# Residual rows of x put straight into the four result tiles of the output stage

## The chip, the cores and the metric

The kernel runs on one core of one Trainium2 chip. The metric is the device time of one execution in microseconds (us). Times inside a profile are counted from the start of its span, which is the time from the first to the last recorded instruction; the execution's own time is a little longer than its span.

## What is computed

One inference step of a one-layer decoder for a prompt of 512 rows and 32 sample rows (8 sequences of 4), each row 1024 wide. Two branches (windowed attention, gated delta rule) are projected, gated and merged; the change lies behind all of that, in the last two lines of the layer:

```python
merged = sigmoid(ga) * (ya @ w_branch_a) + sigmoid(gb) * (yb @ w_branch_b)
r  = ALPHA * x + gate * (merged @ w_out)          # merged: 544 x 1024, w_out: 1024 x 1024
mu = mean(r); var = mean((r - mu)**2)             # over the 1024 columns of a row
y  = (r - mu) * rsqrt(var + LN_EPS) * ln_g + ln_b
```

All values are fp32. Products are made of three passes over high and low parts (high by high, high by low, low by high).

## The kernel before

**How the order comes about.** The kernel first records every operation with the tiles that it reads and writes, and then sets the order of each of five queues with a planner. The queues are TensorE (PE), VectorE (DVE), ScalarE (ACT), GpSimd (POOL) and SyncE (SP), which issues the DMAs. The planner walks through time by its own cost table. On each queue it takes, among the operations whose inputs it reckons ready, the one with the lowest (rank, place in the program). On the chip each queue then runs in that fixed order: an instruction that waits holds back everything behind it on its engine. All recorded operations carry the line L728 in the profile, so they are told apart by their tiles.

**The output stage.** The merged rows stand as `mhi[k]` and `mlo[k]` (eight blocks of 128 columns, high and low part), the weights as `wo0h`, `wo0l` (columns 0 to 511, called half 0 here) and `wo1h`, `wo1l` (half 1). `product_out` makes one product of a block of 128 rows (tt = 0 to 3) and a half n: 24 matmuls of 512 columns into one tile `pp`. There are two `pp` buffers, so PE can begin a product only when the product two before it has been read out of its buffer by DVE. The loop at the end of `body` goes through the products in the order (0,0), (1,0), (2,0), the sample rows, (0,1), (1,1), (2,1), (3,0) and (3,1); the last one is split in two products of 256 columns, called (3,1a) and (3,1b) here.

For each product, `load_x` has SP load 128 x 512 values of x into a tile `xr` and ACT scale them by ALPHA. DVE then writes half the gated product into the result tile `r[tt]` (a `SCALAR_TENSOR_TENSOR r<-pp,gp`) and adds `xr` to it (a `TENSOR_TENSOR r<-r,xr`). `xr` comes from the pool `o2` with two buffers, so a load can begin only when the add two loads before it is done.

When both halves of a block are there, `norm_out` normalises the row. For blocks 0 to 2 ACT makes the mean and the variance (`sq,mv<-r` twice, with small steps between); for block 3 DVE does so (`BN_STATS`, `BN_AGGR`). DVE then subtracts the mean and multiplies by `lng` (1024 columns, `r<-r,mv,lng`), takes a reciprocal, and multiplies and adds `lnb` in two halves (`r<-r,mv,lnb`), each followed by its store to `y_p`. Block 3 has a lower rank number, so it goes ahead of other work that is ready.

`samples_out` handles the 32 sample rows, spread over 128 partitions with 256 columns each. Its loads are `xs`, `lns` and `quarter`; two tiny matmuls with `quarter` (tile `pd`) sum up means and variances and stand in PE's queue between the matmuls of other products.

Of the kernel before, what the change touches and what calls it, by code (L numbers as in the profile page):

```python
# [11 lines left out]
F32 = mybir.dt.float32  # L12
F32R = mybir.dt.float32r
AF = mybir.ActivationFunctionType
OP = mybir.AluOpType
# [4 lines left out]
D = 1024  # L20
# [14 lines left out]
ALPHA = 2.0 ** 0.25  # L35
# [215 lines left out]
class Recorder:  # L251
# [21 lines left out]
    def pool(self, make, name, bufs, side):  # L273
        return Pool(self, make, name, bufs, side)
# [506 lines left out]
def body(ctx, tc, io):  # L781
    rec = Recorder()
    pe, ve, se, ge, sp = rec.engines()
# [104 lines left out]
    n = CONST[2].shape[1]  # L888
# [8 lines left out]
    with ExitStack() as fctx:  # L897
# [65 lines left out]
        for b, (c, m) in enumerate(CHUNKS):  # L963
# [3 lines left out]
            for k in range(c, c + m):  # L967
                se.activation(x1[0][:, k, :SEQ], xT[:, k, :SEQ], AF.Copy, scale=sc[:, k, 0:1])
                if k == c:
# [4 lines left out]
                                        op0=OP.mult, op1=OP.subtract)  # L974
# [3 lines left out]
            for k in range(c, c + m):  # L978
                for t in range(3):
                    w, w_ = (x[:, k - c, 128 * t:128 * t + 128] for x in (hi, lo))  # L980
# [24 lines left out]
        with rec.together():  # L1005
            for k in range(KT):
                q = k % 4
# [1244 lines left out]
    gp = al.tile([128, D], F32, name="gp")  # L2252
# [5 lines left out]
    def out_rows(n, k):  # L2258
        return io["w_out"][k * 128:k * 128 + 256, 512 * n:512 * n + 512].rearrange("(a p) c -> p a c", a=2)

    def load_out(n):

        for k in range(0, KT, 2):
            raw = (wraw if n == 0 or k < 6 else o1).tile([128, 2, 512], F32, name="wo", **({"tag": "wraw"} if n == 0 or k < 6 else {}))
            sp.dma_start(raw, out_rows(n, k))
            plain[n, k] = raw
            se.activation(wo[n][0][:, k:k + 2], raw, AF.Copy)
            ve.tensor_sub(wo[n][1][:, k:k + 2], raw, wo[n][0][:, k:k + 2].bitcast(F32))
# [28 lines left out]
    o1 = pool(ox, "o1", 1, "right")  # L2297
    o2 = pool(ox, "o2", 2, "right")
    wo.append([o1.tile([128, KT, 512], F32R, name=f"wo1{u}") for u in "hl"])
    load_out(1)  # L2300
    lng = o1.tile([128, D], F32, name="lng")
    sp.dma_start(lng, io["ln_g"].to_broadcast([128, D]))
    lnb = o1.tile([128, D], F32, name="lnb")
    sp.dma_start(lnb, io["ln_b"].to_broadcast([128, D]))
    for k in range(0, KT, 2):
        name = ("hi", "lo")[k // 4]
# [7 lines left out]
            sp.dma_start(lns[32 * q:32 * q + 32, i], io[n][:, 256 * q:256 * q + 256].to_broadcast([32, 256]))  # L2314
    quarter = o1.tile([128, 128], F32, name="quarter")
    sp.dma_start(quarter, io["const_q"])
    r = [o1.tile([128, D if tt < 4 else 256], F32, name=f"r{tt}") for tt in range(5)]
    bn, bns = o1.tile([128, 4, 6], F32, name="bn"), o1.tile([128, 6], F32, name="bns")
    parts = lambda k: ((mhi[k], 0), (mhi[k], 1), (mlo[k], 0))

    def product_out(tt, c0, c1):
        n, w = c0 // 512, slice(c0 % 512, c0 % 512 + c1 - c0)
        po = pp()[:, 0:c1 - c0]
        for k in range(KT):
            for i, (a, b) in enumerate(parts(k)):
                pe.matmul(po, a[:, 128 * tt:128 * tt + 128], wo[n][b][:, k, w],
                          start=(k == 0 and i == 0), stop=(k == 7 and i == 2))
        return po

    def load_x(tt, n):  # L2330
        xr = o2.tile([128, 512], F32, name="xr")
        sp.dma_start(xr, io["x"][128 * tt:128 * tt + 128, 512 * n:512 * n + 512])
        se.activation(xr, xr, AF.Copy, scale=ALPHA)
        return xr

    def norm_out(tt, mv=None):
        q = r[tt]
        if mv is None:
            mv, sq = o2.tile([128, 4], F32, name="mv"), o1.tile([128, D], F32, name="sq")
            se.activation(sq, q, AF.Copy, scale=1.0 / D, accum_out=mv[:, 0:1])  # L2340
            se.activation(mv[:, 3:4], mv[:, 0:1], AF.Copy, scale=-1.0)
            se.activation(sq, q, AF.Square, bias=mv[:, 3:4], accum_out=mv[:, 1:2])
            se.activation(mv[:, 2:3], mv[:, 1:2], AF.Sqrt, bias=eps5, scale=1.0 / D)
        else:
            se.activation(mv[:, 2:3], mv[:, 1:2], AF.Sqrt, bias=eps5)
        ve.scalar_tensor_tensor(q, q, mv[:, 0:1], lng, op0=OP.subtract, op1=OP.mult)
        ve.reciprocal(mv[:, 2:3], mv[:, 2:3])
        for w in (slice(0, 512), slice(512, 1024)):
            ve.scalar_tensor_tensor(q[:, w], q[:, w], mv[:, 2:3], lnb[:, w], op0=OP.mult, op1=OP.add)
            sp.dma_start(io["y_p"][128 * tt:128 * tt + 128, w], q[:, w])  # L2350

    def samples_out():
        xr = o1.tile([128, 256], F32, name="xs")
        for b in range(4):
            sp.dma_start(xr[32 * b:32 * b + 32], io["x"][SEQ:NT, 256 * b:256 * b + 256])
        se.activation(xr, xr, AF.Copy, scale=ALPHA)
        po = pp()
        with rec.together():
            for k in range(KT):
                for q in range(4):  # L2360
                    n, c = divmod(256 * q, 512)
                    pe.matmul(po[32 * q:32 * q + 32, 0:256], ms[:, k], plain[n, k // 2 * 2][:, k % 2, c:c + 256],
                              start=(k == 0), stop=(k == 7), tile_position=(0, 32 * q))
        q = r[4]
        ve.scalar_tensor_tensor(q, po[:, 0:256], 0.5, gs, op0=OP.mult, op1=OP.mult)
        ve.tensor_add(q, q, xr)
        ve.bn_stats(bns, q)
        mv = o2.tile([128, 4], F32, name="mv")
        ve.bn_aggr(mv[:, 0:2], bns)
        pm = pd()  # L2370
        pe.matmul(pm[:, 0:1], quarter, mv[:, 0:1], start=True, stop=True)
        se.activation(mv[:, 2:3], pm[:, 0:1], AF.Square, bias=mv[:, 0:1], scale=-1.0)
        ve.tensor_add(mv[:, 1:2], mv[:, 1:2], mv[:, 2:3])
        pe.matmul(pm[:, 1:2], quarter, mv[:, 1:2], start=True, stop=True)
        se.activation(mv[:, 3:4], pm[:, 1:2], AF.Sqrt, bias=eps5)
        ve.tensor_copy(mv[:, 2:3], pm[:, 0:1])
        ve.scalar_tensor_tensor(q, q, mv[:, 2:3], lns[:, 0], op0=OP.subtract, op1=OP.mult)
        ve.reciprocal(mv[:, 3:4], mv[:, 3:4])
        ve.scalar_tensor_tensor(q, q, mv[:, 3:4], lns[:, 1], op0=OP.mult, op1=OP.add)
        for b in range(4):  # L2380
            sp.dma_start(io["y_s"][:, 256 * b:256 * b + 256], q[32 * b:32 * b + 32])

    for tt, n in ((0, 0), (1, 0), (2, 0), (None, 0), (0, 1), (1, 1), (2, 1), (3, 0), (3, 1)):
        if tt is None:
            samples_out()
            continue
        xr, q = load_x(tt, n), r[tt]
        step = 256 if n and tt == 3 else 512
        for c in range(512 * n, 512 * n + 512, step):
            po = product_out(tt, c, c + step)  # L2390
            w = slice(c, c + step)
            at_end = tt == 3 and c == 768
            rec.rank = -2 * (n and tt == 3)
            with rec.together() if at_end else nullcontext():
                ve.scalar_tensor_tensor(q[:, w], po, 0.5, gp[:, w], op0=OP.mult, op1=OP.mult)
                ve.tensor_add(q[:, w], q[:, w], xr[:, c - 512 * n:c - 512 * n + step])
                if tt == 3:
                    for i in range(c // 256, (c + step) // 256):
                        ve.bn_stats(bn[:, i, :], q[:, 256 * i:256 * i + 256])
                if at_end:  # L2400
                    mv = o2.tile([128, 4], F32, name="mv")
                    ve.bn_aggr(mv[:, 0:2], bn.rearrange("p a b -> p (a b)"))
            rec.rank = 0
        if n:
            rec.rank = -2 * (tt == 3)
            norm_out(tt, mv if tt == 3 else None)
            rec.rank = 0
# [112 lines left out]
```

## Time and profile before

| what | value |
|---|---|
| median of 3 runs (lowest to highest) | 882.32 us (881.55 to 884.74) |
| time of the profiled execution | 881.68 us |
| its span | 879.9 us |
| instructions in the span | 20682 |
| busy: PE, PE weight loads, DVE, ACT, POOL | 98%, 92%, 73%, 51%, 8% |
| mean granted TensorE clock | 0.995 |
| output stage, first product read out to the end of the span | 828.54 to 879.9 us |

Rows of the timeline give start, duration, engine, line, operation, output<-inputs, shapes and count; a bracket at the end tells how long the engine had been idle before, and what ended that. Rows with xN merge N neighbours. SPq rows are DMA issues: their duration is the issue, not the transfer. In a row of the windows, each engine has its busy time and its instructions, then come the granted clock, the share of time that the 16 DMA engines were busy, and GB/s.

### The profile page before, as it was taken

To read this page: it belongs to the slowest core of one execution; us is meant where nothing else is said; L and a number is where in the kernel's file an instruction comes from. 1 tells how busy PE (TensorE), PEld (TensorE's weight loads), DVE (VectorE), ACT (ScalarE), POOL (GpSimd) and SP (SyncE) were. 2 spreads that over 40 slices of the span, in tenths; PEclk is the share of its full clock that TensorE was granted. 3 is DMA by queue.
4 is the path that set the end of the run, shared out by engine and by line. 5 is a ranking of instruction groups with operands and counts; after the bars stand their busy time and mean duration, and the time that the engine had idled before them with its cause. 6 is when DMAs were issued, how large, how long until landed. Compare 5 with 4: busy or idle time off the path is not lost.

```text
span 879.9 us, 20682 instructions
## 1 busy us (share of the span) xinstructions
PE 859.4 (98%) x8152; PEld 811.3 (92%) x8152; DVE 643.4 (73%) x1328; ACT 452.0 (51%) x1073; POOL 70.2 (8%) x167
## 2 busy tenths in 40 slices
PE   8999999999999999999999999999999999999995
PEld 7889999898999899999999998999999999999874
DVE  4776557565448999867999853556999699998547
ACT  3556656765546796347785446732442222334333
POOL 0120110110001110001020000021010000001000
PEclk9999999999999999999999999999999999999998
DMA  9976769656687887899878796479969799987974
GB/s 331 348 218 205 232 205 285 227 194 224 191 262 253 276 275 205 269 288 305 303 227 283 238 303 216 171 214 300 345 213 381 271 412 417 372 293 238 342 250 153
DMA packets 121069, 236.18 MB, mean 268 GB/s; under 512 B 49174, under 2 KB 76640, under 8 KB 118284
## 3 DMA queue, kind: packets, MB, share of 16 engines
q1 hardware_dynamic: 120972, 234.86, 79.6%
q8 instruction: 64, 1.05, 0.5%
q14 instruction: 33, 0.27, 0.1%
HBM read 218.53 MB, written 103.97 MB: 367 GB/s over the span
## 4 chain that ended last, share of the span: by engine, by line
PE 79%; DVE 7%; DMA 6%; ACT 5%; issue 1%; SPq 1%; POOL 0%; DVEq 0%; ACTq 0%
PE pp L728 60%; PE pg L728 8%; PE pd L728 7%; PE pb L728 4%; ACT L728 1%; DMA wv<-dw 1%; DMA slab<-in_ks 1%; DMA dO<-orow 1%; ACT hi L728 1%; DMA bias<-in_bias_p 1%; DVE r L728 1%; ACT sq L728 1%; DVE acc L728 1%; DMA wc<-in_w_cb 1%; DMA S<-in_state_delta 1%
## 5 line engine op out<-in xcount | busy, mean ns | idle before, releaser
L728 PE MATMUL pp<-hhi,hi 128*128 128x272 f32 x1360 | 397.6, 292 | 2.0 <-DVE zt L728 1.3
L728 PE MATMUL pp<-hhi,lo 128*128 128x272 f32 x1360 | 397.3, 292 | 0.0
L728 PE MATMUL pp<-hlo,hi 128*128 128x272 f32 x1360 | 395.7, 291 | 0.0
L728 PEld LDWEIGHTS pp<-hhi,hi 128*128 128x128 f32 x1360 | 256.4, 189 | 4.9 <-issue 1.8
L728 PEld LDWEIGHTS pp<-hhi,lo 128*128 128x128 f32 x1360 | 256.4, 189 | 2.1 <-issue 1.4
L728 PEld LDWEIGHTS pp<-hlo,hi 128*128 128x128 f32 x1360 | 256.3, 188 | 1.4 <-issue 0.4
L728 ACT ACTIVATE hi<-wt 128x1024 fp32r<-128x1024 f32 (+1 forms) x101 | 103.5, 1025 | 169.4 <-PE pp L728 138.3
L728 DVE TENSOR_TENSOR lo<-wt,hi 128x1024 fp32r<-128x1024 f32 (+1 forms) x101 | 118.9, 1177 | 73.9 <-ACT hi L728 73.4
L728 DVE SCALAR_TENSOR_TENSOR acc<-ext,cw,acc 128x568 f32<-128x568 f32 x72 | 57.9, 805 | 1.6 <-ACT acc L728 0.6
L728 DVE TENSOR_TENSOR slab<-slab 128x512 f32<-128x512 f32 (+1 forms) x66 | 43.0, 668 | 7.1 <-DMA slab<-in_ks 3.9
L728 DVE TENSOR_REDUCE slab<-slab 128x8 f32<-128x512 f32 (+2 forms) x66 | 42.7, 659 | 3.3 <-ACT slab L728 2.9
L728 ACT ACT_TABLE_LOAD x32 | 41.1, 1283 | 4.2 <-DMA dO<-orow 1.7
L728 ACT ACTIVATE zt<-pp 128x272 f32<-128x272 f32 x48 | 18.7, 389 | 37.7 <-PE pp L728 36.3
L728 PE MATMUL pp<-ybh,lo 128*128 128x272 f32 x128 | 36.9, 288 | 0.0
L728 PE MATMUL pp<-ybh,hi 128*128 128x272 f32 x128 | 36.9, 288 | 0.0
L728 PE MATMUL pp<-ybl,hi 128*128 128x272 f32 x128 | 36.8, 287 | 0.0
L728 ACT ACTIVATE P<-P,st 128x256 f32<-128x256 f32 (+1 forms) x64 | 31.1, 488 | 10.9 <-DVE st L728 10.8
L728 POOL COPY cx<-ext 128x3 f32<-128x3 f32 (+1 forms) x48 | 22.4, 496 | 151.9 <-ACT ext L728 124.5
L728 DVE CUSTOM_DVE_ANT_0 P<-pg,bias 128x256 f32<-128x256 f32 (+1 forms) x64 | 23.0, 402 | 13.3 <-PE pg L728 13.2
L728 PEld LDWEIGHTS pp<-ybh,hi 128*128 128x128 f32 x128 | 24.1, 189 | 0.2
L728 ACT ACTIVATE spare<-pp 128x272 f32<-128x272 f32 (+1 forms) x32 | 16.3, 510 | 15.5 <-PE pp L728 15.5
L728 PEld LDWEIGHTS pp<-ybh,lo 128*128 128x128 f32 x128 | 24.1, 188 | 0.1
(421 smaller groups left out, 1539.5 us busy)
## 6 DMA issues: line engine op xcount, KB each, us to landing
out_kv_s<-in_cache SPq DMA_DIRECT2D x144, 512.0 KB
wt<-in_w_in SPq DMA_DIRECT2D x85, 512.0 KB
out_kv_s<-in_cache SPq DMA_DIRECT2D x24, 496.0 KB
wc<-in_w_cb SPq DMA_DIRECT2D x16, 512.0 KB
slab<-in_ks SPq DMA_DIRECT2D x32, 256.0 KB
slab<-in_vs SPq DMA_DIRECT2D x32, 256.0 KB
kv<-in_ks SPq DMA_DIRECT2D x16, 512.0 KB
kv<-in_vs SPq DMA_DIRECT2D x16, 512.0 KB
```

The lines of the kernel that those rows point to most:

```text
L728: getattr(real[x.engine], x.name)(*map(arg, x.args), **{k: arg(v) for k, v in x.kw.items()})
```

## The change

The result tiles `r` are made earlier in the program, directly after the last part of `w_out` is loaded. Four loads of 128 x 1024 bring x's rows into `r[0]` to `r[3]`, and ACT scales them there. `load_x` and `xr` are gone. For each product DVE writes the gated product into a tile `gated` (pool `o2`, two buffers) and adds it to `r[tt]` in place.

```diff
     load_out(1)
+    r = [o1.tile([128, D if tt < 4 else 256], F32, name=f"r{tt}") for tt in range(5)]
+    for tt in range(4):
+        sp.dma_start(r[tt], io["x"][128 * tt:128 * tt + 128])
+        se.activation(r[tt], r[tt], AF.Copy, scale=ALPHA)
     lng = o1.tile([128, D], F32, name="lng")
...
-    r = [o1.tile([128, D if tt < 4 else 256], F32, name=f"r{tt}") for tt in range(5)]
...
-    def load_x(tt, n):
-        xr = o2.tile([128, 512], F32, name="xr")
-        sp.dma_start(xr, io["x"][128 * tt:128 * tt + 128, 512 * n:512 * n + 512])
-        se.activation(xr, xr, AF.Copy, scale=ALPHA)
-        return xr
...
-        xr, q = load_x(tt, n), r[tt]
+        q = r[tt]
...
-                ve.scalar_tensor_tensor(q[:, w], po, 0.5, gp[:, w], op0=OP.mult, op1=OP.mult)
-                ve.tensor_add(q[:, w], q[:, w], xr[:, c - 512 * n:c - 512 * n + step])
+                gated = o2.tile([128, 512], F32, name="gated")[:, 0:step]
+                ve.scalar_tensor_tensor(gated, po, 0.5, gp[:, w], op0=OP.mult, op1=OP.mult)
+                ve.tensor_add(q[:, w], q[:, w], gated)
```

The planner orders all five queues anew. Up to the output stage nothing moves on any of them. POOL's queue is the same throughout. On PE the products keep their order.

SP's queue at the start of the output stage (a row names the tile, its number and its source; - is before, + is now):

```order
 L728 DMA out_kv_s<-in_cache 16x8192
 L728 DMA wo<-in_w_out 128x2x512
+L728 DMA r_11175<-in_x 128x1024
+L728 DMA r_11181<-in_x 128x1024
+L728 DMA r_11184<-in_x 128x1024
+L728 DMA r_11190<-in_x 128x1024
 L728 DMA lng<-in_ln_g 128x1024
 L728 DMA lnb<-in_ln_b 128x1024
```

The four loads of x's rows stand right behind the last part of `w_out` and ahead of `lng`, `lnb`, the eight `lns`, `quarter` and the four `xs`; the eight `xr` loads further down are gone.

DVE's queue before, from the read-out of product (3,0) to that of (3,1b):

```order
L728 SCALAR_TENSOR_TENSOR r3_11463<-pp_11415,gp_10704 128x512
L728 SCALAR_TENSOR_TENSOR r1_11208<-r1_11208,mv_11444,lng_11175 128x1024
L728 RECIPROCAL mv_11444<-mv_11444 128x1
L728 SCALAR_TENSOR_TENSOR r1_11208<-r1_11208,mv_11444,lnb_11181 128x512 x2
L728 SCALAR_TENSOR_TENSOR r3_11463<-pp_11459,gp_10704 128x256
L728 SCALAR_TENSOR_TENSOR r2_11245<-r2_11245,mv_11471,lng_11175 128x1024
L728 TENSOR_TENSOR r3_11463<-r3_11463,xr_11449 128x256
L728 RECIPROCAL mv_11471<-mv_11471 128x1
L728 TENSOR_TENSOR r3_11463<-r3_11463,xr_11441 128x512
L728 BN_STATS bn_11531<-r3_11463 128x6
L728 SCALAR_TENSOR_TENSOR r2_11245<-r2_11245,mv_11471,lnb_11181 128x512 x2
L728 BN_STATS bn_11531<-r3_11463 128x6 x2
```

The same stretch of DVE's queue now, again from the read-out of (3,0), with that of (3,1b) as the last row:

```order
L728 SCALAR_TENSOR_TENSOR gated_11471<-pp_11420,gp_10704 128x512
L728 SCALAR_TENSOR_TENSOR r2_11184<-r2_11184,mv_11438,lnb_11208 128x512 x2
L728 TENSOR_TENSOR r3_11190<-r3_11190,gated_11471 128x512
L728 BN_STATS bn_11502<-r3_11190 128x6
L728 SCALAR_TENSOR_TENSOR gated_11507<-pp_11466,gp_10704 128x256
L728 BN_STATS bn_11502<-r3_11190 128x6
L728 TENSOR_TENSOR r3_11190<-r3_11190,gated_11507 128x256
L728 BN_STATS bn_11502<-r3_11190 128x6
L728 SCALAR_TENSOR_TENSOR gated_11531<-pp_11499,gp_10704 128x256
```

The normalisation of block 1 and the `lng` step of block 2 have moved ahead of the read-out of (3,0).

PE's queue now, around the two `quarter` matmuls of the samples (`pp_11325` is product (1,1), `pp_11370` is (2,1)); before, the two stood after the second and the seventh matmul of (1,1):

```order
L728 MATMUL pp_11325<-wo1l_11186,mhi_11145 128x512
L728 MATMUL pd_11367<-mv_11361,quarter_11308 128x1
L728 MATMUL pp_11325<-wo1h_11169,mlo_11152 128x512
L728 MATMUL pp_11370<-wo1h_11169,mhi_10772 128x512
L728 MATMUL pp_11370<-wo1l_11186,mhi_10772 128x512
L728 MATMUL pp_11370<-wo1h_11169,mlo_10787 128x512
L728 MATMUL pp_11370<-wo1h_11169,mhi_10813 128x512
L728 MATMUL pp_11370<-wo1l_11186,mhi_10813 128x512
L728 MATMUL pp_11370<-wo1h_11169,mlo_10824 128x512
L728 MATMUL pd_11367<-mv_11361,quarter_11308 128x1
```

The first now stands behind 23 of the 24 matmuls of (1,1), the second behind the sixth matmul of (2,1).

## The prediction

> **What bounds the kernel now.** I read the page first, then the stages behind the last product in a table of windows, then the chain that ended last, and then the timeline of each engine there.
>
> ```profile
> span 879.9 us, 20682 instructions
> ...
> PE 859.4 (98%) x8152; PEld 811.3 (92%) x8152; DVE 643.4 (73%) x1328; ACT 452.0 (51%) x1073; POOL 70.2 (8%) x167
> ```
>
> PE is the bound nearly everywhere, so a change that moves nothing ahead of the output stage can only win what PE waits there, and what is left once PE is through.
>
> ```profile
> 850.00:865.00 15.00, 15.00 (x70) 12.26 (x69) 7.47 (x13) 8.23 (x17) 0.00 (x0) 1.00 0.77 250
> 865.00:870.00 5.00, 4.71 (x42) 4.51 (x40) 4.96 (x9) 3.81 (x9) 0.00 (x0) 1.00 0.29 110
> 870.00:872.00 2.00, 0.00 (x0) 0.00 (x0) 2.00 (x5) 0.00 (x0) 0.00 (x0) 0.99 0.00 0
> 872.00:874.00 2.00, 0.00 (x0) 0.00 (x0) 1.90 (x6) 0.00 (x0) 0.00 (x0) 0.50 0.71 266
> ```
>
> PE is full until just short of 870 and does nothing behind that. DVE is half busy from 850 to 865 (7.47 of 15 us) and full from 865 on: its work is bunched at the end. The chain says the same:
>
> ```profile
> 859.84 4.44 PE pp L728 x19
> ...
> 864.92 1.28 DVE r L728
> ...
> 876.27 0.66 DVEq L2511
> ```
>
> It leaves PE at 864.28, some 5 us before PE's end, and stays with DVE. The timeline shows why.
>
> ```profile
> 854.00 1.46 DVE L728 TENSOR_TENSOR r<-r,xr 128x512 f32<-128x512 f32 x2 [0.17 <-ACT xr L728]
> ...
> 859.60 1.29 ACT L728 ACTIVATE xr<-xr 128x512 f32<-128x512 f32 x2 [1.11 <-DMA xr<-in_x]
> ...
> 861.38 1.28 DVE L728 TENSOR_TENSOR r<-r,xr 128x512 f32<-128x512 f32 x2
> ...
> 864.92 1.28 DVE L728 SCALAR_TENSOR_TENSOR r<-r,mv,lng 128x1024 f32<-128x1024 f32 x1
> ...
> 866.30 1.42 DVE L728 SCALAR_TENSOR_TENSOR r<-r,mv,lnb 128x512 f32<-128x512 f32 x2
> ...
> 867.97 1.27 DVE L728 SCALAR_TENSOR_TENSOR r<-r,mv,lng 128x1024 f32<-128x1024 f32 x1
> ...
> 869.43 0.28 PE L728 MATMUL pp<-wo1h,mlo 128*128 128x256 f32 x1
> ...
> 869.57 0.67 DVE L728 TENSOR_TENSOR r<-r,xr 128x512 f32<-128x512 f32 x1
> ...
> 870.49 1.40 DVE L728 SCALAR_TENSOR_TENSOR r<-r,mv,lnb 128x512 f32<-128x512 f32 x2
> ...
> 871.81 0.74 DVE L728 BATCH_NORM_STATS2 bn<-r 128x6 f32<-128x256 f32 x2
> ...
> 872.47 0.41 DVE L728 SCALAR_TENSOR_TENSOR r<-pp,gp 128x256 f32<-128x256 f32 x1
> ...
> 875.52 1.41 DVE L728 SCALAR_TENSOR_TENSOR r<-r,mv,lnb 128x512 f32<-128x512 f32 x2
> ```
>
> The adds of `xr` run in pairs (854.00, 861.38), because only two loads fit and each pair waits for the one before. So the second half of block 1, whose product PE ended at about 853, is added at 861.4, and the norms of blocks 1 and 2 (864.92 to 871.8) stand in DVE's queue in front of the last product. PE ends at 869.43 + 0.28 = 869.71; DVE reads that product out at 872.47. These **2.7 us** are the backlog. From 872.47 on block 3 runs without a hole to its last store, 7.4 us to the end of the span.
>
> **The change part by part.** *DVE.* Each product still costs one read-out and one add, of the same shapes; the sum does not change, only the order. In the new order, from the read-out of (3,0) at 864.31 on, DVE has by the pitch of the rows: read-out 0.61, two `lnb` halves 1.4, add 0.6, statistics 0.35, read-out 0.35, statistics 0.35, add 0.44, statistics 0.43; together 4.5 us, done at 868.8, before PE's end at 869.71. Then the read-out of (3,1b) waits for PE and starts at 869.75 instead of 872.47: a gain of 2.7 us. That holds only if the norm of block 1 and the `lng` step of block 2 are done by 864.3. From the read-out of (1,1) at 852.9 until 864.3 DVE has two read-outs and two adds (4 x 0.61), three `lng` (3.6), four `lnb` (2.7), and the samples and small steps (about 1.9, an estimate from the same stretch before): 10.6 us in 11.4. So there are 0.8 us of room in front of (3,0) and 0.95 behind it.
>
> *ACT.* Block 2's mean must be there at 862.8. One block takes ACT this long:
>
> ```profile
> 855.49 1.07 ACT L728 ACTIVATE sq<-r 128x1024 f32<-128x1024 f32 x1 [0.76 <-DVE r L728]
> ...
> 858.19 0.29 ACT L728 ACTIVATE mv<-mv,eps 128x1 f32<-128x1 f32 x1
> ```
>
> All of it takes 3.0 us (855.49 to 858.48), and the mean is there about half way. Block 1's add ends about 855.7 (ACT 855.8 to 858.8), block 2's about 860.0 (mean 861.5, root 863.1): in time. Eight scalings of 512 become four of 1024 and stand behind the last weight split, where ACT is idle anyway; they cost nothing as long as the loads are there.
>
> *DMA.* Four loads of 512 KB now stand ahead of `lng`; eight of 256 KB later on are gone. When does what stands in that place land?
>
> ```profile
> 827.70 0.44 SPq L728 DMA_DIRECT2D lng<-in_ln_g  x1
> ...
> 831.31 0.31 SPq L728 DMA_DIRECT2D lns<-in_ln_g  x1
> ...
> 833.27 0.31 SPq L728 DMA_DIRECT2D lns<-in_ln_g  x1
> ...
> 834.52 1.59 SPq L728 DMA_DIRECT2D lns<-in_ln_b  x2
> ...
> 835.80 1.06 ACT L728 ACTIVATE wo1h<-wo 128x1024 fp32r<-128x1024 f32 x1 [3.43 <-DMA wo<-in_w_out]
> ...
> 837.47 1.87 SPq L728 DMA_DIRECT2D lns<-in_ln_b  x2
> ...
> 839.39 0.42 SPq L728 DMA_DIRECT2D quarter<-in_const_q  x1
> ...
> 839.85 0.91 SPq L728 DMA_DIRECT2D xr<-in_x  x2
> ...
> 842.20 0.42 SPq L728 DMA_DIRECT2D xs<-in_x  x1
> ...
> 844.35 0.42 ACT L728 ACTIVATE xs<-xs 128x256 f32<-128x256 f32 x1 [0.26 <-DMA xs<-in_x]
> ```
>
> And in the list of waits, SP's own:
>
> ```profile
> SPq L728 <- DMA lng<-in_ln_g: 1.3, 1, 1.3
> SPq L728 <- DMA lnb<-in_ln_b: 1.2, 1, 1.2
> ```
>
> The last weights landed at 835.8, `lng` at 837.47 (SP waited for it with the seventh `lns`) and `lnb` one such wait later, at 839.04: 1.6 us per 512 KB. So r0 lands at about 837.5, r1 839.0, r2 840.6, r3 842.2, then `lng` 843.8 and `lnb` 845.4, 6.3 us later than before. `lng` is first used at 854: hidden. Behind them SP issues `quarter` (839.39 + 6.3 = 845.7) and `xs`, the last at 842.20 + 6.3 less 1.0 for the two `xr` issues that stood between, 847.5; at the 2.15 us that `xs` took before, it is there at **849.6** instead of 844.3. No row shows whole rows of x being loaded. The bounds come from the earlier `lns` issues, each of which waited for one 512 KB transfer: 833.27 less 831.31, 1.96 us for a weight load, and 834.52 less 833.27, 1.25 for a copy of the cache. I take `lng`'s, the same shape in the same place. At the upper bound `xs` is there at 851.2.
>
> *The new waits.* `gated` has two buffers, so the read-out of (2,0) now waits for the add of (0,0), and that for r0: landed 837.5, scaled 838.5, added 839.2, read-out over at 839.9 (before: 838.4).
>
> ```profile
> 837.74 0.69 DVE L728 SCALAR_TENSOR_TENSOR r<-pp,gp 128x512 f32<-128x512 f32 x1 [3.74 <-PE pp L728]
> ...
> 841.22 0.50 PE L728 MATMUL pp<-wo1h,mhi 128*128 128x512 f32 x1
> ...
> 846.90 0.39 PE L728 MATMUL pp<-wo1h,mhi 128*128 128x512 f32 x1
> ...
> 847.36 0.28 PE L728 MATMUL pd<-mv,quarter 128*128 128x1 f32 x2
> ...
> 852.93 0.40 PE L728 MATMUL pp<-wo1h,mhi 128*128 128x512 f32 x1
> ```
>
> PE wants that buffer for (0,1) at 841.22: 1.3 us of room. The other wait is PE's on the samples. (1,1) begins at 846.90; with 0.233 us a matmul the first `quarter` matmul comes up at 852.25, the second at 854.1. From `xs` to the end of its statistics was under 1.6 us before (one scaling, one add, two statistics, 0.4, 0.4, 0.4 and 0.2 with the gaps), so the first can run at 851.2. The second needs ACT, which does block 0's mean and square (2.7) in between: 849.6 + 0.5 + 2.7 + 0.26 for ACT's step and 0.2 for DVE's gives 853.3. Both are in time, by 1.0 and 0.8 us. At the upper bound of the loads the second is late by 0.8 us and PE with all that follows.
>
> **The sum.** 2.7 us less backlog, nothing added: span 877.2, time of that execution 879.0. The median shown lies 0.6 above the profiled execution; from it the same sum gives 879.6. Of the four known times three lie from 881.55 to 882.32, so I take 879.3. That is 0.3% less; about 0.5% (4.4 us) is what a measurement of this kernel can tell from no change, its three runs already being 0.36% apart.
>
> **The rivals.** *B: PE waits for the samples.* `xs`, `quarter` and `lns` lie behind 2 MB more. For it speaks that the second slot has only 0.8 us of room; against it, `lng`'s rate. At the upper bound PE loses 0.8 us (880.1); if `xs` comes 3 us late, at 852.6, it loses 2.2 and 0.5 is left (881.5). I put it at 881. [...]
>
> *C: the backlog stays in part.* If ACT's block 1 starts 2 us later than I reckon, block 1's norm slides behind (3,0) again and about 1.5 us of the 2.7 come back: 880.8. Against it: the 0.8 and 0.95 us of room, both of which it would have to eat.
>
> *D: slower than before.* One mechanism: r0 lands late, the add of (0,0) holds `gated`, the read-out of (2,0) holds its `pp` buffer, and PE waits at 841.2 with 28 us of products behind it. Each us that r0 lands after 838.8 costs one. It turns the sign at 841.5, four us later than `lng` landed in that place, and costs over 0.5% from 845.9 on. Beyond about 2 us such a wait costs more than itself: PE's last matmul ended at 869.71, and the clock row falls from 0.99 (870 to 872) to 0.50. So a wait of 3 us would let the following matmuls start at half clock and could cost 3 us more: 885. [...]
>
> *E: more than 2.7.* The 7.4 us from the last read-out on are a fixed chain of block 3, so there is nothing more to win but scatter.
>
> **How the numbers follow.** A (forecast, 878 to 880.5) 0.68, B 0.15, C 0.09, D 0.05, E 0.03. Nearly all of A, B and C lies within 0.5% (877.9 to 886.7). Scatter and E put 0.08 under it; a severe D 0.03 above. The range takes in A's scatter, the fast bound of the base (881.55 - 2.7 = 878.85, less 1) and B and C with half of the 2.4 us by which one run before lay higher: 877.8 to 882.8.
>
> **What would show it.** In the changed profile, the read-out of (3,1b) starts within 0.1 us of PE's last matmul, the span from there to the end is still 7.4 us, and DVE is busier between 850 and 865. r0 is scaled at 837 to 839. PE has no hole at 841 and none in front of a `quarter` matmul. A hole there shows B or D; a read-out that lags PE shows C. The prediction is wrong if the loads of x's rows run slower than 2 us each, or if ACT's norms come later than DVE's places for them.

## The result, and the profile after

| what | before | changed |
|---|---|---|
| median of 19 runs each (lowest to highest) | 882.69 us (879.75 to 887.01) | 880.47 us (877.71 to 882.17) |
| ratio, 95% interval | | 0.997 (0.9956 to 0.9984) |
| span of the profiled execution | 879.9 us | 876.5 us |
| first read-out of the output stage | 828.54 | 827.07 |
| output stage, first read-out to the end of the span | 51.36 us | 49.43 us |

The change is worth 0.3%: the interval leaves out 1 and the direction is the one forecast, but it is less than the 0.5% that the prediction named for calling a difference. The stage won 1.93 us. The other 1.47 us between the two spans lie ahead of it, where no instruction moved: they are scatter between executions. So a time of the changed profile compares with one of before after adding 1.47.

The page's head and the windows of the changed kernel, with the edges used before:

```profile
span 876.5 us, 20668 instructions
...
PE 859.6 (98%) x8152; PEld 811.5 (93%) x8152; DVE 643.1 (73%) x1328; ACT 451.2 (51%) x1069; POOL 69.6 (8%) x167
```

```profile
850.00:865.00 15.00, 15.00 (x79) 12.63 (x78) 12.43 (x23) 8.12 (x18) 0.00 (x0) 1.00 0.74 253
865.00:870.00 5.00, 3.27 (x29) 3.07 (x28) 3.87 (x11) 0.02 (x1) 0.00 (x0) 1.00 0.28 105
```

DVE's busy time, third among the engines, was 7.47 us between 850 and 865 and is 12.43. In the next 5 us it fell from 4.96 to 3.87. With the edges moved by the 1.47 us (848.53 to 863.53, and on to 868.53) it is 11.24 and 4.01, which is the fairer comparison. The same work (643 us in both) has moved forward, under PE's cover. The chain that ended last (start, duration, what) now stays with PE to the last product:

```profile
852.96 15.32 PE pp L728 x90
868.28 0.02 issue
868.30 0.44 DVE gated L728
...
871.38 0.75 DVE r L728
872.13 0.66 DVEq L2509
```

And the timeline of the same place:

```profile
862.87 0.69 DVE L728 SCALAR_TENSOR_TENSOR gated<-pp,gp 128x512 f32<-128x512 f32 x1
...
866.96 0.43 DVE L728 BATCH_NORM_STATS2 bn<-r 128x6 f32<-128x256 f32 x1
867.99 0.28 PE L728 MATMUL pp<-wo1h,mlo 128*128 128x256 f32 x1
868.30 0.42 DVE L728 SCALAR_TENSOR_TENSOR gated<-pp,gp 128x256 f32<-128x256 f32 x1 [0.92 <-PE pp L728]
...
871.38 1.42 DVE L728 SCALAR_TENSOR_TENSOR r<-r,mv,lnb 128x512 f32<-128x512 f32 x2
```

PE's last matmul ends at 867.99 + 0.28 = 868.27 and DVE reads the product at 868.30, after 0.92 us of idleness that PE ended. Before, DVE came 2.76 us late; now 0.03. But from that read-out to the end of the span it is 8.2 us where it was 7.4: 0.73 of the 2.73 us won was lost again after DVE's end. Where, the experiments show.

### The profile page after: what moved, and what is told of

Same layout as the page of the kernel before. It is cut to its first block, busy times and chain, and to the rows that moved or that the text cites. A ratio compares the mean times of both kernels' runs of the same rounds, so it can differ in the third digit from the quotient of the medians.

```text
span 876.5 us, 20668 instructions
## 1 busy us (share of the span) xinstructions
PE 859.6 (98%) x8152; PEld 811.5 (93%) x8152; DVE 643.1 (73%) x1328; ACT 451.2 (51%) x1069; POOL 69.6 (8%) x167
## 4 chain that ended last, share of the span: by engine, by line
PE 84%; DVE 5%; ACT 4%; DMA 4%; issue 1%; SPq 1%; POOL 0%; DVEq 0%; ACTq 0%
PE pp L728 64%; PE pg L728 9%; PE pd L728 8%; PE pb L728 4%; ACT L728 1%; DMA slab<-in_ks 1%; DMA dO<-orow 1%; DMA wc<-in_w_cb 1%; DMA wv<-dw 1%; DVE slab L728 1%; ACT sq L728 1%; DVE acc L728 1%; ACT hi L728 1%; DVE lo L728 1%; SPq L728 1%
```

## The experiments

Every profile below is read by four numbers: PE's part of the stage (first read-out to PE's last matmul), the lag of the last read-out behind PE, the tail from DVE's end to the end of the span, and the whole stage. Read-out of (3,1b) to DVE's end was 4.46 to 4.50 us in all of them. Spans are printed to 0.1 us, so a tail and a stage are good to 0.05 us. Each ratio is to runs of the kernel before that were taken beside it; the medians come from several chips.

| kernel | PE's part | lag | tail | stage | median, us | ratio to before, 95% |
|---|---|---|---|---|---|---|
| before | 41.17 | 2.76 | 2.97 | 51.36 | | |
| changed | 41.20 | 0.03 | 3.70 | 49.43 | 880.47 | 0.9956 to 0.9984 |
| changed, again | 41.20 | 0.04 | 3.76 | 49.49 | 881.36 | 0.9972 to 1.0007 |
| xr, 4 buffers | 41.13 | 0.04 | 3.59 | 49.25 | 881.79 | 0.9971 to 1.0006 |
| xr, 3 buffers | 41.17 | 1.15 | 2.98 | 49.78 | 880.81 | 0.9953 to 0.9985 |
| three more adds | 41.21 | 2.18 | 3.74 | 51.60 | 882.21 | 0.9977 to 1.0011 |
| late loads | 41.87 | 0.04 | 3.72 | 50.11 | 880.56 | 0.9966 to 1.0005 |
| late loads, 5 gated | 41.22 | 0.03 | 3.69 | 49.42 | 881.25 | 0.9965 to 1.0002 |
| eight halves | 41.20 | 0.03 | 3.15 | 48.88 | 880.53 | 0.9957 to 1.0006 |
| lng, lnb in 4 parts | 41.21 | 0.04 | 3.41 | 49.13 | 880.05 | 0.9950 to 0.9987 |
| lng, lnb in 7 parts | 41.23 | 0.03 | 3.15 | 48.89 | 879.34 | 0.9951 to 0.9982 |
| 1 gated | 43.20 | 0.04 | 3.74 | 51.46 | 883.16 | 0.9998 to 1.0029 |
| late loads, 1 gated | 52.53 | 0.17 | 3.70 | 60.86 | 891.40 | 1.0075 to 1.0125 |

Only the last row's time is more than 0.5% from before. The intervals don't tell the others apart; the profiles do, since the parts of the stage repeat to about 0.1 us where nothing touches them.

**The changed kernel again**, in a measurement of its own:

> The changed kernel once more, beside the kernel before on the same chip. Theory (the backlog on DVE behind PE's end is gone): ratio 0.996 to 0.998, and in the profile the read-out of (3,1b) starts within 0.1 us of PE's last matmul, against some 2.7 us before; PE's last matmul as far behind the first read-out of the stage as before. If the gain were scatter of the stages ahead, the ratio is 1.000 and PE's end moves instead.

The stage repeats to 0.06 us (49.49) and the lag is 0.04. The ratio, 0.999, missed the expected 0.996 to 0.998 and can't be told from 1, so these whole times don't confirm the gain; the stage does. The span of this profile is 882.4, with the first read-out at 832.91, so executions differ ahead of the stage by more than the change is worth.

**Was it the two `xr` buffers?** The kernel before, with more of them and nothing else of the change:

```diff
-        xr = o2.tile([128, 512], F32, name="xr")
+        xr = o2.tile([128, 512], F32, name="xr", bufs=4)
```

> The kernel before, with four buffers of xr in place of two; nothing is loaded into the result tiles, and there is no tile for the gated product. Theory (two buffers of xr made the adds and so the norms of blocks 0 to 2 late): the whole gain comes with it, ratio 0.996 to 0.998, read-out of (3,1b) within 0.3 us of PE's end. Rival (it is the early loading of whole rows, or the add in place): no gain, ratio 0.999 to 1.001, read-out 2 us or more behind PE's end.

The timeline of that kernel, last matmul and last read-out:

```profile
869.80 0.28 PE L728 MATMUL pp<-wo1h,mlo 128*128 128x256 f32 x1
...
870.12 0.42 DVE L728 SCALAR_TENSOR_TENSOR r<-pp,gp 128x256 f32<-128x256 f32 x1 [0.94 <-PE pp L728]
```

PE ends at 870.08, the read-out follows 0.04 us later. Two more buffers do what the whole change does in the stage (49.25). The ratio, 0.9989, missed the expected range here too and can't be told from 1; the lag is what decides against the rival. With `bufs=3`:

> The kernel before with three buffers of xr. Theory: the third load of a group no longer waits for the first add; block 0 and 1 are still added in a pair behind the read-out of (1,1), but block 2 no longer waits. The read-out of (3,1b) lags PE's end by 0 to 1 us, ratio 0.997 to 0.999. Rival (early whole rows): as before, lag 2.7 us, ratio 1.000.

```profile
872.61 0.28 PE L728 MATMUL pp<-wo1h,mlo 128*128 128x256 f32 x1
...
874.04 0.41 DVE L728 SCALAR_TENSOR_TENSOR r<-pp,gp 128x256 f32<-128x256 f32 x1
```

One more buffer leaves 1.15 us of lag, a little more than expected. The lag shrinks with each buffer, 2.76, 1.15, 0.04: the ring of two was the cause.

**Does the backlog cost what it lasts?** The changed kernel with three more adds on DVE behind block 2's norm (a sum that nothing reads):

```diff
+        if tt == 2:
+            spare_sum = o1.tile([128, D], F32, name="spare_sum")
+            rec.rank = -3
+            for _ in range(3):
+                ve.tensor_add(spare_sum, q, lnb)
+            rec.rank = 0
```

> The changed kernel with three more additions of 128 x 1024 on DVE behind the norm of block 2, into a tile that nothing reads: they stand between the add of (3,0) and the statistics of block 3. Theory (what counts is DVE's backlog at PE's end): 3 x 1.21 us of work against 0.9 us in which DVE waited there, so the read-out of (3,1b) lags PE's end by 2.7 us again and the time is that of the kernel before, ratio 0.999 to 1.001. Rival (the gain is from the DMAs or from PE): 0.997 as the changed kernel.

```profile
868.13 1.22 DVE L728 TENSOR_TENSOR spare_sum<-r,lnb 128x1024 f32<-128x1024 f32 x1
...
870.73 0.28 PE L728 MATMUL pp<-wo1h,mlo 128*128 128x256 f32 x1
...
872.21 1.07 DVE L728 BATCH_NORM_STATS2 bn<-r 128x6 f32<-128x256 f32 x3
873.19 0.41 DVE L728 SCALAR_TENSOR_TENSOR gated<-pp,gp 128x256 f32<-128x256 f32 x1
```

The lag came back: 2.18 us, and the stage is 2.17 longer than the changed kernel's. It is less than the 2.7 expected because the adds advance DVE by 1.14 each (not 1.22), and the three statistics now run as one row, without gaps. The backlog costs one for one.

**Does it matter that the loads stand in front?** The changed kernel with the four loads and scalings moved behind `quarter`:

```diff
-    for tt in range(4):
-        sp.dma_start(r[tt], io["x"][128 * tt:128 * tt + 128])
-        se.activation(r[tt], r[tt], AF.Copy, scale=ALPHA)
     lng = o1.tile([128, D], F32, name="lng")
...
     sp.dma_start(quarter, io["const_q"])
+    for tt in range(4):
+        sp.dma_start(r[tt], io["x"][128 * tt:128 * tt + 128])
+        se.activation(r[tt], r[tt], AF.Copy, scale=ALPHA)
```

> The changed kernel with the four loads and scalings of x's rows behind quarter instead of ahead of lng; gated still has two buffers. Theory (the loads are hidden only because they stand first; rival D's mechanism): r0 is scaled some 15 us after the stage's first product is read out instead of 9.4 (836.48 less 827.07), so the add of (0,0), the read-out of (2,0) behind it and PE's product (0,1) all come late. PE shows a hole of 3 to 5 us at the start of (0,1), where the changed kernel has none. The stage from its first read-out to the end of the span grows from 49.4 us to 53 to 54 if the hole costs only itself, and to 56 to 57 if the clock row falls as it did 2.3 us behind PE's last matmul in the kernel before. Time 885 to 889. Rival (where the loads stand makes no difference, DVE's order hides it): no hole over 0.5 us, stage 49.4, time as the changed kernel.

```profile
841.67 0.42 DVE L728 SCALAR_TENSOR_TENSOR r<-pp,gs 128x256 f32<-128x256 f32 x1 [2.83 <-PE pp L728]
842.24 0.47 PE L728 MATMUL pp<-wo1h,mhi 128*128 128x512 f32 x1 [0.64 <-DVE r L728]
...
844.14 1.06 ACT L728 ACTIVATE r<-r 128x1024 f32<-128x1024 f32 x1 [6.56 <-DMA r<-in_x]
...
845.23 0.69 DVE L728 TENSOR_TENSOR r<-r,gated 128x512 f32<-128x512 f32 x1 [3.14 <-ACT r L728]
...
845.96 0.69 DVE L728 SCALAR_TENSOR_TENSOR gated<-pp,gp 128x512 f32<-128x512 f32 x1
```

r0 was as late as expected (844.14 less the first read-out at 828.79 is 15.4), and the read-out of (2,0) too (845.96). But PE waited only 0.64 us: my expectation missed. The planner had put the samples' read-out (841.67) ahead of the add of (0,0), and (0,1) began at 842.24, when the samples had left their buffer and (2,0) was still unread. I had not followed this new order. The same with `bufs=5` for `gated`:

> As the kernel with the late loads, but gated has five buffers, so a read-out need not wait for an add. Theory (the hole comes from the two buffers of gated, not from the DMA itself): no hole at (0,1), PE's part of the stage 41.2 us again, lag of the last read-out behind PE's end at most 0.5 us, stage 49.4 to 50. Rival (the adds are late whatever the buffers, and DVE's bunch comes back at the end): PE's part stays 41.2, but the read-out of (3,1b) lags by 1 to 3 us and the stage is 50.5 to 52.5.

No wait of PE in the stage, 49.42: the 0.64 us came from the two `gated` buffers, as the theory had it, and with buffers enough late loads cost nothing.

**Rival D at full size.** One `gated` buffer, with the loads in front and with the loads late:

```diff
-                gated = o2.tile([128, 512], F32, name="gated")[:, 0:step]
+                gated = o2.tile([128, 512], F32, name="gated", bufs=1)[:, 0:step]
```

> The changed kernel with one gated buffer instead of two; the loads of x's rows stay in front. Now the read-out of (1,0) must wait for the add of (0,0), and the samples' product wants the pp buffer of (1,0). Theory (rival D's chain: add, gated, pp, PE): the add of (0,0) ends 11.3 us behind the stage's first read-out, the read-out of (1,0) 12.0 behind it, and PE, which wants the buffer at 9.2, waits 2.8 us ahead of the samples. If that wait costs only itself, PE's part of the stage is 44.0 instead of 41.2 and the stage 52.2 instead of 49.4. If the clock falls after 2.3 us as behind PE's last matmul in the kernel before, the matmuls behind the hole are slower for some us and the stage is 53.5 to 55.5. Rival (the planner's new order hides the one buffer): no hole over 0.5 us, PE's part 41.2 to 41.7. Time 883 to 888 by the theory.

> The kernel with the late loads of x's rows, and one gated buffer: rival D in full. r0 is scaled 16.4 us behind the first read-out, as in the kernel with late loads and two buffers. Theory: add over at 17.1, read-out of (1,0) over at 17.8, PE, which wants the buffer at 9.2, waits 8.6 us ahead of the samples; the quarter matmuls come early in (0,1) and may wait for xs for 0 to 3 us more. PE's part of the stage 49.8 to 53 if holes cost only themselves, 53 to 57 if the clock falls in the hole and stays low for some us (the clock row below 0.9 behind the hole would show it). Stage 58 to 66, time 890 to 897, slower than before by 1 to 1.7%. Rival (such chains are hidden by PE's other work): stage under 53, time within 0.5% of before.

The read-out of (1,0) and the first matmul of the samples, with the loads in front:

```profile
838.87 0.69 DVE L728 SCALAR_TENSOR_TENSOR gated<-pp,gp 128x512 f32<-128x512 f32 x1
...
839.66 0.41 PE L728 MATMUL pp<-hi,ms 128*32 128x256 f32 x2 [1.91 <-issue]
```

With the loads late:

```profile
845.87 0.69 DVE L728 TENSOR_TENSOR r<-r,gated 128x512 f32<-128x512 f32 x1 [6.64 <-ACT r L728]
846.67 0.69 DVE L728 SCALAR_TENSOR_TENSOR gated<-pp,gp 128x512 f32<-128x512 f32 x1
...
847.46 0.64 PE L728 MATMUL pp<-hi,ms 128*32 128x256 f32 x2 [9.29 <-issue]
```

The windows of that last kernel (the granted clock is third from the end):

```profile
838.00:840.00 2.00, 0.17 (x1) 0.00 (x0) 1.22 (x1) 0.00 (x0) 0.00 (x0) 1.00 0.24 72
840.00:842.00 2.00, 0.00 (x0) 0.00 (x0) 0.00 (x0) 0.00 (x0) 0.00 (x0) 0.80 0.19 58
842.00:844.00 2.00, 0.00 (x0) 0.00 (x0) 0.00 (x0) 0.00 (x0) 0.00 (x0) 0.50 0.94 293
...
848.00:850.00 2.00, 2.00 (x25) 0.99 (x21) 1.48 (x3) 1.36 (x2) 0.00 (x0) 0.50 1.31 515
850.00:852.00 2.00, 2.00 (x28) 1.17 (x24) 0.06 (x1) 1.06 (x2) 0.00 (x0) 0.64 0.83 336
852.00:854.00 2.00, 2.00 (x24) 1.27 (x17) 0.78 (x2) 0.00 (x0) 0.00 (x0) 1.00 1.20 410
```

The chain add, `gated`, `pp`, PE is real: PE begins 0.10 us after the end of the read-out of (1,0) in both (839.56 and 847.36), though the list of waits puts its idle time down to "issue". With early loads it costs 1.91 us and no clock: PE's part is 43.20, 2.0 more. I had expected 2.8; in this execution r0 came earlier, and ACT scaled it 8.4 us behind the first read-out (836.93 less 828.54) instead of 9.4. With late loads PE waits 9.29 us, and the clock is at 0.5 from 841.2 (the 0.80 row) to 851.4 (the 0.64 row). PE worked at half clock from 847.46 to 851.4, which costs half of that: 41.2 + 9.3 + 2.0 = 52.5, and PE's part is 52.53. That lies in the range expected for holes that cost only themselves (49.8 to 53), though the clock did fall; the hole was 0.7 us longer than expected, and the clock cost less than that expectation gave it. The kernel is 1.0% slower than before.

**Smaller loads.** The changed kernel with x's rows loaded and scaled in eight halves:

```diff
-        sp.dma_start(r[tt], io["x"][128 * tt:128 * tt + 128])
-        se.activation(r[tt], r[tt], AF.Copy, scale=ALPHA)
+        for w in (slice(0, 512), slice(512, 1024)):
+            sp.dma_start(r[tt][:, w], io["x"][128 * tt:128 * tt + 128, w])
+            se.activation(r[tt][:, w], r[tt][:, w], AF.Copy, scale=ALPHA)
```

> The changed kernel with x's rows loaded and scaled in eight halves of 128 x 512 in the same early place. [...] By my reading of the trace this buys nothing, since PE has no hole there: PE's part of the stage 41.2 us, lag 0.0 to 0.1. SP gets four more DMA issues: if the 8 KB instruction transfer that stands 0.3 us ahead of the end of the changed kernel belongs to SP's program, it moves ahead by several instructions, and the stretch from DVE's end to the end of the span falls from 3.7 to 3.0 us, stage 48.7. If that stretch has another cause, 3.6 to 3.8 and stage 49.4.

```profile
837.74 1.06 ACT L728 ACTIVATE wo1h<-wo 128x1024 fp32r<-128x1024 f32 x1 [3.43 <-DMA wo<-in_w_out]
838.71 4.97 ACT L728 ACTIVATE r<-r 128x512 f32<-128x512 f32 x8
```

The first half is scaled 8.9 us behind the first read-out (829.82), 0.5 earlier than the whole row in the changed kernel's first profile (9.4). But that count depends on when the last weights land: the other profiles that load whole rows in front have 8.4 to 9.2. Counted from the start of the last weight split (837.74 here, 835.14 in the changed kernel) the half begins after 0.97 us and the whole row after 1.34 (1.33 to 1.35 in the others). So the half lets ACT begin 0.37 us sooner, without idling. PE's part stays 41.20: PE was not waiting for it. The tail shrank, though, from 3.70 to 3.15.

**Where the tail's 0.7 us went.** I first suspected an 8 KB instruction transfer that falls 0.24 us ahead of the end in the changed kernel and 6.24 ahead before. Two kernels bear on this and on the other candidate, the place of the last store in SP's list of final waits, for which the second was made. They load `lng` and `lnb` in 2 + 2 and in 4 + 3 parts, two and five DMA issues more:

```diff
-    sp.dma_start(lng, io["ln_g"].to_broadcast([128, D]))
+    for w in (slice(0, 512), slice(512, 1024)):
+        sp.dma_start(lng[:, w], io["ln_g"][:, w].to_broadcast([128, 512]))
```

> The changed kernel with lng and lnb each loaded in two halves of 512 columns: two DMA issues more on SP, and nothing else moves on any engine. Theory (the tail of the changed kernel is 0.7 us longer than that of the kernel before because an 8 KB instruction transfer falls between the last store and the last instructions of SP): the transfer falls earlier, at least 2 us ahead of the end, DVE's end to the end of the span takes 3.0 us (up to 3.6 if it falls on the last stores themselves), stage 48.7. Rival (the 0.7 us are scatter of the last store, or the transfer is another engine's): it stays 0.3 us ahead of the end, 3.7 us, stage 49.4. Lag 0.0 to 0.1 in both. The whole time moves by under 0.1% and can't tell them apart; the profile can.

> The changed kernel with lng loaded in four parts and lnb in three: five DMA issues more on SP. The DMAs of SP signal eight semaphores in turn, and at the end SP goes through these in a fixed order. The trace's semaphore records show the last store on the sixth in that order in the kernel before (0.19 us from its wait to SP's last step), on the first in the changed kernel (0.91 us, five more waits behind it), on the third with two issues more (0.67), on the fifth with four more (0.20). Five more put it on the last. Theory (the tail's 0.7 us come from the place of the last store's semaphore in that list): DVE's end to the end of the span takes 2.9 to 3.0 us instead of 3.7, stage 48.6 to 48.8, lag 0.0 to 0.1. Rival (it is the 8 KB instruction transfer near the end): the tail follows where that transfer falls, and is 3.4 or more if it falls within 0.3 us of the end.

SP's waits in the last 7 us, before:

```profile
SPq L2511 <- DMA out_y_p<-r: 1.5, 2, 0.8
```

In the changed kernel:

```profile
SPq L2509 <- DMA out_y_p<-r: 1.7, 1, 1.7
```

With seven parts:

```profile
SPq L2511 <- DMA out_y_p<-r: 1.3, 2, 0.8
```

In the traces of the kernel before and of the changed one, each of SP's DMAs (767 and 763) signals the next of eight semaphores in turn, and at the end SP goes through them in one order, the same in both, in six steps. The trace's semaphore records of SP give this (times in us; issues are counted against the changed kernel; place is that of the last store's semaphore among the six steps):

| kernel | issues | place | issue of last store to its wait over | wait over to the end | 8 KB transfer ahead of the end |
|---|---|---|---|---|---|
| changed | 0 | first | 2.08 | 1.61 | 0.24 |
| lng, lnb in 4 parts | +2 | third | 2.04 | 1.37 | 0.26 |
| before | +4 | fifth | 2.04 | 0.89 | 6.24 |
| eight halves | +4 | fifth | 2.20 | 0.90 | 1.44 |
| lng, lnb in 7 parts | +5 | last | 2.24 | 0.83 | 1.32 |

(The expectation above calls before's place the sixth; it is the fifth.) In the changed kernel SP gets past the last store's semaphore first and then still has five steps to go; before, four of the six had passed while the store was under way, and one was left. The time from that wait to the end goes with the place and not with the transfer: with two more issues the transfer stays at 0.26 and the stretch shrinks all the same (its tail, 3.41, is neither the 3.0 of the theory nor the 3.7 of the rival). With late loads the transfer falls behind the end of the span, and the tail is 3.72 as in the changed kernel.

The steps alone do not make the 0.72 us between 1.61 and 0.89. By SP's records a step whose semaphore was signalled long before takes some 0.07 us, so four more of them make 0.28. Another 0.31 is a pause: at one place of this list SP goes on after 0.35 us instead of some 0.04, though what the next step waits for was signalled over 6 us earlier. In the changed kernel the pause stands behind the six steps, ahead of a `DRAIN` that takes 0.13 us there and 0.01 before: the last 0.11. With two more issues it stands ahead of the fifth step, in eight halves ahead of the third, with seven parts ahead of the second, so one step earlier for each issue. Before, none shows. In eight halves and in seven parts it falls while the last store is under way and costs nothing. So the four DMA issues that the change saves cost 0.72 us at the end, because steps and a pause of SP come to stand behind the last store's wait. Why SP pauses stays open. The expectation of seven parts, 2.9 to 3.0 us, was missed by 0.1 to 0.15: there the wait itself took 2.24 instead of 2.04. It is longer in the profiles whose 8 KB transfer falls 1.3 to 2.5 us ahead of the end (2.54 in that of four `xr` buffers); that this transfer is the reason was not tried by itself.

No version beats the changed kernel by a measurable amount. The one with seven parts has one of the two shortest stages, 48.89, and the lowest median, 879.34, but its stage is shorter by 0.54 us, 0.06% of the whole time.

## Why the prediction was right, step by step

- *DVE*, right. It put the read-out of (3,0) at 864.31 and DVE's end ahead of PE at 868.8; with 1.47 added the rows give 864.34 and 868.86. The lag fell from 2.76 to 0.03 where 2.7 us were promised. Adding buffers and adding work both moved the lag as this step says.
- *DMA*, right but on the slow side. ACT began r0 at 836.48 and r3 at 840.37:

```profile
836.48 1.06 ACT L728 ACTIVATE r<-r 128x1024 f32<-128x1024 f32 x1 [0.28 <-DMA r<-in_x]
...
840.37 1.06 ACT L728 ACTIVATE r<-r 128x1024 f32<-128x1024 f32 x1 [0.35 <-DMA r<-in_x]
847.29 0.42 ACT L728 ACTIVATE xs<-xs 128x256 f32<-128x256 f32 x1 [5.86 <-DMA xs<-in_x]
```

That is 1.30 us per 512 KB, near the lower bound of 1.25 and not `lng`'s 1.6. Only r0 was late: scaled at 839.01 by the old count (836.48 + 1.06 + 1.47) where 838.5 was forecast. `xs` is there at 848.76 by the old count, 0.8 earlier than forecast.
- *The new waits*, right. No wait of PE is listed in the stage. The `quarter` matmuls ran at 850.82 and 852.68, which is 852.29 and 854.15 by the old count; forecast were 852.25 and 854.1. Rival B did not happen. The read-out of (2,0) ended at 840.58 by that count instead of 839.9, 0.5 of it from r0, which came that much later, and the rest from the gaps between the rows: half of the 1.3 us of room was used.
- *ACT* and rival C, right: the lag is nil, so the norms were in time.
- *The sum*: the step that failed is "the 7.4 us from the last read-out on are a fixed chain". DVE's part of it was (4.46 and 4.50), the rest was not: 2.97 became 3.70. The term was mis-sized because a DMA issue saved early was priced at nothing at the end. With it the stage gains 1.9, and the median of the 19 runs before less that gives 880.8; 880.5 was measured, 1.2 above the forecast. The forecast also stood on 882.0 for the kernel before (879.3 + 2.7), and 19 runs gave 882.69. Two errors of 0.7 add up here, less 0.3 that no run explains, and the result lies just inside the upper edge of A's 878 to 880.5. The interval of the ratio is 2.5 us wide, so it is the stage and not the whole time that bears out the sum.
- *Rival D* was right as a mechanism with one `gated` buffer, and partly in its price. With two buffers "each us that r0 lands after 838.8 costs one" was not seen: r0 some 6 us later cost 0.64, because the planner's order changed with the loads. A hole of 1.9 us cost only itself, one of 9.3 cost 2.0 more. But its "beyond about 2 us" comes from the fall of the clock 2.25 us behind PE's last matmul in the kernel before (869.71 to 871.96), and that is no constant: it is 3.05 in the hole of the kernel with late loads and one buffer (838.17 to 841.22), and 3.57 behind the changed kernel's last matmul (the clock record has the fall at 871.84).

## What to carry to other kernels

Where a ring of small buffers ties late adds to early loads, look for the work that it bunches on the engine behind the last product: only the part that outlasts the bound engine can be won, here 2.7 of 880 us, and one more buffer or two may do as much as a new data flow. Price the end of the program as well as the place of the change: saving four DMA issues moved the last store and a pause in SP's final list of waits, and that gave 0.7 us back. When a change is worth less than the scatter of whole runs, measure the stage by its own marks in the profile.

## What the runs showed of the hardware

In the thirteen profiles' records the granted clock fell to 0.5 anywhere from 2.03 us (four `xr` buffers) to 5.21 us (late loads, five `gated`) after the last matmul of the program. In the stage, with the hole of 9.29 us (late loads, one buffer) it was at 0.5 for 10.24 us, from 841.2 to 851.4, and the hole of 1.91 us (one `gated` buffer, loads in front) left it at 1.00. Three of the profiles (the changed kernel's second, three more adds, three `xr` buffers) have one stretch of 3.41 us at half clock far ahead of the output stage. The windows of the changed kernel's second profile:

```profile
292.00:294.00 2.00, 1.06 (x9) 0.87 (x8) 1.11 (x2) 0.13 (x1) 0.00 (x0) 1.00 1.11 435
294.00:296.00 2.00, 0.08 (x1) 0.09 (x2) 2.00 (x10) 0.74 (x3) 0.26 (x2) 1.00 0.72 291
296.00:298.00 2.00, 2.00 (x13) 1.96 (x14) 1.97 (x6) 1.98 (x8) 0.00 (x0) 0.73 0.44 164
298.00:300.00 2.00, 2.00 (x11) 2.00 (x11) 2.00 (x4) 0.72 (x2) 0.00 (x0) 0.50 1.10 371
300.00:302.00 2.00, 2.00 (x16) 1.86 (x16) 0.79 (x3) 1.45 (x4) 0.00 (x0) 0.91 0.47 120
```

Its waits of PE between 280 and 302:

```profile
PE pg L728 <- ACT P L728: 2.9, 1, 2.9
```

PE waited 2.9 us for ACT there (0.8 in the first profile of the same kernel, which keeps its clock), and 3.41 us behind it ran at half clock, up to 1.7 us lost (an estimate, half of 3.41). In the other two profiles PE's longest listed wait near the fall is 1.3 (three `xr` buffers) and 1.5 us (three more adds), where the changed kernel has 0.6. Both are shorter than the hole of 1.91 us that left the clock at 1.00, so what makes it fall was not shown. Such a stretch is one part of the scatter ahead of the stage. It is not all of it: first read-outs of profiles without such a stretch range from 827.07 to 830.31. What the rest is stays open.
